# The gated rows of the one-hot matrices: one VectorE compare-and-multiply per token instead of a compare and a ScalarE scaling

## The chip, the cores and the metric

The program runs on one core of a Trainium2 chip. A core has TensorE (PE: matrix products, with a weight load PEld ahead of each), VectorE (DVE), ScalarE (ACT), GpSimd (POOL) and SyncE (SP, which here only issues transfers); 16 DMA engines move data between HBM and the on-chip memory SBUF. TensorE writes its results to PSUM. The metric is the device time of one execution in microseconds, lower is better.

## The reference, cut to what matters

Two transformer blocks run over 512 tokens of width 1024 (retention, sliding-window attention, then latent and differential attention). The change concerns the last part, a mixture of 16384 one-neuron experts (`peer_ffn`). For every token and each of 8 heads it picks 16 experts; an expert number is made of two halves below 128, and each pick has a gate `g`.

```
cand = sv[:, :, 0, :, None] + sv[:, :, 1, None, :]
fv, fpos = lax.top_k(cand, PEER_TOPK)
eidx = jnp.take_along_axis(cidx, fpos, axis=-1)      # first half * 128 + second half
g = jax.nn.softmax(fv, axis=-1)
a = jax.nn.gelu(jnp.einsum('ted,td->te', u_tab[eidx], hb))
return jnp.einsum('te,ted->td', g * a, v_tab[eidx])
```

## The kernel before, in words

The first 1050 us are the attention layers, the next 180 the router's scores and the first picks. What matters here is the stretch from about 1230 to 1770 us of the profile, called the gate stage below, and the 560 us behind it, the V stage.

Tokens come in four tiles of 128. Tile 0's experts are gathered row by row: `gather` (L1239, an indirect DMA issued by POOL) fetches one row per token, and `weigh` (L1248, VectorE) multiplies it with the token. For the other three tiles (384 tokens, 96 groups of four) TensorE works out the activations of all experts, 128 at a time, and a dense matrix of gates, which the V stage multiplies together before the sum over experts.

In the gate stage one loop runs over `n`, the 96 groups of four tokens. For each n it records, in this order: `one_hots(n + 4)`, some pieces of `finalize` (top-16 picks, gates and numbers of the next tile, L1139 to L1207), about 1.03 steps of `u_mm` and `u_prep`, 1.33 gathers and weighings, and `dense_gates(n)`.

- `u_prep` prepares the table rows of 128 experts: a load on SP's queue (L1044, two experts' blocks, 1 MB), a rounded copy `hi` on ScalarE (L1052), and the rest `lo` = raw - hi (L1056), in turn on VectorE (one step) and on POOL (two halves). `u_mm` is 24 products `pa` on TensorE (L94), then a gelu on ScalarE (L1071, `gsp`) which also frees the PSUM buffer (there are two), and a store `Ad` on SP's queue.
- `one_hots` builds, for four tokens, two matrices with a row per pick: entry (row, i) is one where i equals the half of the pick's number, and in the second matrix it is the gate instead of one. VectorE compares the row of numbers 0 to 127 (`io`) with both halves of all four tokens in one step of 128x1024 (L1213, `junk`), then ScalarE multiplies the second matrix of each token by its gates (L1216, four steps of 128x128).
- `dense_gates` multiplies the two matrices of each token on TensorE (`att`, four products) and copies the result on ScalarE (L1230) into staging buffers, written to HBM (`Gd`, L1232) every eighth n. The staging buffers and the loads of `u_prep` share four buffers, `raw`.

The order on PE and on DVE is the order of the loop (`manual_schedule`); the orders on ACT, POOL and SP come from the framework's scheduler, which may place them anew when instructions go. There are four `junk` buffers, so one_hots(n + 4) waits for the products of dense_gates(n). The loop is

```
lr[n + AQ] = one_hots(n + AQ)
...
    u_mm()
    u_prep(nc.vector if nl % 2 else nc.gpsimd)
gathers(NG1 * (n + 1) / NQ)
...
dense_gates(n, lr.pop(n))
```

Of the kernel before, what the change touches and what calls it, by code (L numbers as in the profile page):

```python
# [31 lines left out]
def consts():  # L32
    """Tables that depend on the shapes alone."""
    f = np.float32
    out = {}
    ang = (1.0 / (f(10000.0) ** np.linspace(0.0, 1.0, 128, dtype=f))).astype(f)
    pos = np.arange(S, dtype=f)
    a = (pos[None, :] * ang[:, None]).astype(f).astype(np.float64)
    out["xcos"] = np.cos(a).astype(f)
    out["xsin"] = np.sin(a).astype(f)  # L40
    gam = 1.0 - 2.0 ** (-5.0 - np.arange(4, dtype=np.float64))
    diff = np.arange(S)[None, :] - np.arange(P)[:, None]
    dec = np.where(diff[:, None, :] >= 0, gam[None, :, None] ** np.maximum(diff, 0)[:, None, :], 0.0) / 16.0
    out["dec"] = dec.astype(f)
    half = 32
    inv = (1.0 / (f(10000.0) ** (np.arange(half, dtype=f) / f(half)))).astype(f)
    a = (np.arange(S, dtype=f)[:, None] * inv[None, :]).astype(f).astype(np.float64)
    out["rcos"] = np.cos(a).astype(f)
    out["rsin"] = np.sin(a).astype(f)
    d = np.arange(384) - 127  # L50
    dd = np.maximum(d, 0)
    big = 16 + (np.log(np.maximum(dd, 1).astype(f) / f(16)) / f(math.log(128 / 16)) * f(16)).astype(np.int32)
    bucket = np.where(dd < 16, dd, np.minimum(big, 31))
    oh = np.zeros((64, 384), f)
    ok = (d >= 0) & (d < 128)
    for u in range(384):
        if ok[u]:
            oh[bucket[u], u] = 1.0
        else:
            oh[32, u] = NEG  # L60
    out["oneh"] = oh
    out["cmask"] = np.where(np.arange(P)[None, :] <= np.arange(P)[:, None], 0.0, NEG).astype(f)
    out["iota"] = np.broadcast_to(np.arange(P, dtype=f), (P, P)).copy()
    starts = np.cumsum([0] + [16 // (a + 1) for a in range(15)])
    out["iota16"] = np.broadcast_to(np.stack([np.arange(16), starts]).astype(f), (P, 2, 16)).copy()
    return out
# [3 lines left out]
def tile_kernel(ctx: ExitStack, tc: tile.TileContext, I: dict, out: bass.AP):  # L70
# [41 lines left out]
    def rstd(ss, n, inv, eps=EPS, tag="rs"):  # L112
        """(ss * inv + eps) ** -0.5 for [P, n]."""
        m = sm.tile([P, 8], F32, tag="ms", name=nm("ms"))
        r = sm.tile([P, 8], F32, tag=tag, name=nm("rs"))
        nc.gpsimd.tensor_scalar(m[:, :n], ss, inv, eps, op0=OP.mult, op1=OP.add)
        last_rstd[0] = nc.gpsimd.tensor_tensor(r[:, :n], m[:, :n], mhalf[:, :n], op=OP.pow).ins
        return r
# [44 lines left out]
    def wchunk(*a, **kw):  # L163
        """Weights [nk k-tiles, n columns] as exact high and low float32r parts, a list of
        (hi, lo) by k-tile. parts: list of (dram AP [nk*128, c], column offset)."""
        for ks in wload(*a, **kw):
            pass
        return ks

    def gemm_tok(xh, xl, ks, n, t):  # L170
        """psum [128 tokens of tile t, n] = x^T . W"""
        ps = pmm.tile([P, 512], F32, tag="mm", name=nm("mm"))
        nk = len(ks)
        for k, (h, l) in enumerate(ks):
            xs = slice(t * P, (t + 1) * P)
            mm(ps[:, :n], xl[:, k, xs], h[:, :n], k == 0, False)
            mm(ps[:, :n], xh[:, k, xs], l[:, :n], False, False)
            mm(ps[:, :n], xh[:, k, xs], h[:, :n], False, k == nk - 1)
        return ps

    def gemm_T(xh, xl, ks, c0):
        """psum [128 columns of W from c0, all tokens]"""
        ps = pmm.tile([P, 512], F32, tag="mm", name=nm("mm"))
        nk = len(ks)
        cs = slice(c0, c0 + P)
        for k, (h, l) in enumerate(ks):
            mm(ps, l[:, cs], xh[:, k, :], k == 0, False)
            mm(ps, h[:, cs], xl[:, k, :], False, False)
            mm(ps, h[:, cs], xh[:, k, :], False, k == nk - 1)
        return ps  # L190

    def gemm_half(ps, xh, xl, ks, c0, t2):
        """As gemm_T, for two of the tiles of tokens."""
        xs = slice(t2 * 256, t2 * 256 + 256)
        cs = slice(c0, c0 + P)
        nk = len(ks)
        for k, (h, l) in enumerate(ks):
            mm(ps[:, xs], l[:, cs], xh[:, k, xs], k == 0, False)
            mm(ps[:, xs], h[:, cs], xl[:, k, xs], False, False)
            mm(ps[:, xs], h[:, cs], xh[:, k, xs], False, k == nk - 1)  # L200
# [7 lines left out]
    def to_T(src, n, th, tl, t, k0=0):  # L208
        """Transposes src [128 tokens, n*128] into th/tl[:, k0.., tile t]."""
# [24 lines left out]
    def col_vec(ap, n, name):  # L234
        """A vector of n*128 as [128, n], element k*128+p at (p, k)."""
        tl = cst.tile([P, n], F32, name=name)
        nc.gpsimd.dma_start(tl, ap.rearrange("(k p) -> p k", p=P))
        return tl

# [32 lines left out]
    def mod_gain(g_ap, sh_row, sc_row, raw=None):  # L272
        """Row 0: gain * (1 + scale), row 1: shift."""
# [18 lines left out]
    with ExitStack() as sa:  # L292
# [32 lines left out]
        # small vectors and tables of the later stages, loaded when the norms are done  # L325
# [43 lines left out]
        def small():  # L369
            # attention bias by distance, to be read back one row per query  # L370
# [10 lines left out]
            # -lambda on every partition  # L381
# [12 lines left out]
        def a_qk(h):  # L394
            # q, k with the pairs of a rotation in two blocks
# [34 lines left out]
        def a_scores(h, qT, kT):  # L430
            # decayed scores, keys on the partitions
# [71 lines left out]
    with ExitStack() as sb:  # L503
# [53 lines left out]
        def b_scores(g, t, hf, bt, qT, rq):  # L557
            """Softmax of 4 heads, not yet divided by its sum."""
# [99 lines left out]
    with ExitStack() as sc_:  # L658
# [19 lines left out]
        # rope tables with the gains in them: [P, tile, 64] for cos and for sin with its sign  # L678
        tabs = {}

        def rope(dst, src, name, t, n):
            """dst, src [P, n, 64] (normalised, gain not yet applied)."""
# [41 lines left out]
        # rotary key and differential v  # L724
# [15 lines left out]
        def latent(name, c0, nb, lh, ll):  # L740
            """Latents, transposed, and the reciprocal rms of each token."""
# [13 lines left out]
        # latent queries, keys and values  # L755
# [98 lines left out]
        def c_scores(i, h):  # L854
            """Weights of the keys for heads 0..3 (latent, to be divided by the sum) and 4..7."""
# [35 lines left out]
        def c_end(i, h, po, rl4):  # L891
# [4 lines left out]
            else:  # L896
                # rms over a head, where a sum of squares beyond float32's range gives zero
# [14 lines left out]
        # short rows of scores next to long ones  # L912
# [58 lines left out]
        def r_scores(hp, qT, sk, s):  # L971
            """Scores of a half of a head's keys, and the 16 largest."""
# [9 lines left out]
        for c in range(2):  # L982
            cs = slice(c * 512, (c + 1) * 512)
            ks = wchunk([(I["w_out_2"][0][:, cs], 0)], KT, 512, [None] * 4 + [gsub[:, 0:1]] * 4)
            if c == 1:
                gsh = mod_gain(I["norm2_g_2"][0], 3, 4, pc.tile([P, 2 * D], F32, tag="qnT", name="gsh2"))
                # the router's first head fills the wait for the last norm
# [24 lines left out]
    # Tile 0's experts are gathered row by row; for the other tiles all experts' activations  # L1012
    # are worked out on the tensor engine, and weighted by a dense matrix of gates.
# [3 lines left out]
    # activations kept on chip, and rows under way  # L1017
    LA = 14
    NGR = 4
    # the other activations are kept in DRAM  # L1020
# [13 lines left out]
    # activations of all experts, 128 of them (one first half) at a time  # L1034
# [95 lines left out]
    # pairs (a, b) of the two sorted halves that can be among the 16 largest sums  # L1130
    PAIRS = [(0, 1, 16), (1, 2, 8), (2, 3, 5), (3, 4, 4), (4, 5, 3), (5, 8, 2), (8, 16, 1)]

    def finalize(t):
        """Gates and the two halves of the expert numbers, [tokens, slots]; in pieces."""
# [29 lines left out]
        # steps from one a to the next, of its number and of 128 times its first position  # L1164
# [44 lines left out]
    def one_hots(n):  # L1209
        """Both halves of 4 tokens' numbers as rows of ones and zeros, the first times the gates."""  # L1210
        src, tk = iT[n * 4 // P], n * 4 % P
        LR = junk().rearrange("p (e t n) -> p e t n", e=2, t=4)
        nc.vector.tensor_tensor(LR, io.unsqueeze(1).unsqueeze(1).to_broadcast([P, 2, 4, P]),  # L1213
                                src[:, 0:2, tk:tk + 4].unsqueeze(3).to_broadcast([P, 2, 4, P]), op=OP.is_equal)
        for i in range(4):
            nc.scalar.activation(LR[:, 1, i], LR[:, 1, i], AF.Copy, scale=src[:, 2, tk + i:tk + i + 1])  # L1216
# [4 lines left out]
    def dense_gates(n, LR):  # L1221
        """For 4 tokens, [second half of the number, first half]; written by 32."""
# [35 lines left out]
    # shared out over the steps  # L1258
# [3 lines left out]
    def gathers(n, pool_ins=None, dve_ins=None):  # L1262
        """Gathers rows until n of them are under way, and weighs those of the last call."""
# [125 lines left out]
    def step(j):  # L1389
        """Ahead: the loads of a later j; then the sums over this j's experts."""  # L1390
# [17 lines left out]
    with tc.manual_schedule(engines={mybir.EngineType.PE}):  # L1408
# [15 lines left out]
        # the last sums by tile, so that only the last tile's end is left  # L1424
# [12 lines left out]
def layouts(inputs):  # L1437
    """Inputs once more, in another order of their elements."""
# [24 lines left out]
```

## Time and profile before

| what | value |
|---|---|
| median of 3 runs | 2336.23 us (2334.72 to 2336.91) |
| span of the profiled execution, first to last instruction | 2333.6 us |
| busy in the span | PE 2230.1 us (96%), DVE 1587.2 (68%), ACT 984.4 (42%), POOL 767.1 (33%) |
| mean granted TensorE clock | 0.984 of full speed |

Of the profiled execution the span alone is given; the runs of the table are timed without a profile, and their median lies 2.6 us above it. Busy times are averages over stages; which engine a stage waits for is read from that stage. "Start to start" below is the distance between the starts of two neighbouring instructions of one engine: on VectorE the next one's start is shown some 0.08 us before the end of the one ahead of it, so this distance, not the duration, is what an instruction costs in a full queue.

### The profile page before, as it was taken

The page shows a single profiled execution, that of the slowest core. Times are in us where ns is not written, and L with a number is a line of the kernel's source. Part 1 is how long each engine was busy: PE and PEld are TensorE (multiplying, and loading weights), DVE is VectorE, ACT ScalarE, POOL GpSimd, SP SyncE. Part 2 cuts the span into 40 slices and gives each one's busy share as a digit, 9 for nine tenths or more (in the row PEclk, how much of TensorE's full clock was granted, in tenths as well). Part 3 has the DMA queues.
Part 4 walks back from the last instruction along what each step waited for, and adds up shares of the span by engine and source line. Part 5 has one row for each costly group of instructions (what it writes and reads, how often), then busy time and mean ns, then how long its engine had stood idle before and what let it go on. Part 6 is the DMA issues. An engine that isn't in the chain of part 4 may idle for free.

```text
span 2333.6 us, 31094 instructions
## 1 busy us (share of the span) xinstructions
PE 2230.1 (96%) x11343; PEld 1913.5 (82%) x11343; DVE 1587.2 (68%) x2929; ACT 984.4 (42%) x1972; POOL 767.1 (33%) x683
## 2 busy tenths in 40 slices
PE   7999999998989999989999989989999999999999
PEld 6777777787878775678989989989998888888887
DVE  5664545346366665559788797787775888787778
ACT  4213132245353545433436656566653333333332
POOL 4211111111101340000584675585563333222222
PEclk9999999999999999899999999999999999999999
DMA  7754544321212221123346889879999999999995
GB/s 222 188 169 103 155 114 126 90 91 55 72 45 72 91 69 40 43 77 118 118 149 234 325 281 337 294 280 331 333 338 320 354 347 344 343 336 333 337 312 179
DMA packets 226600, 476.33 MB, mean 204 GB/s; under 512 B 15504, under 2 KB 118352, under 8 KB 223376
## 3 DMA queue, kind: packets, MB, share of 16 engines
q1 hardware_dynamic: 121904, 291.79, 37.0%
q0 software_dynamic: 38160, 134.90, 16.7%
q10 hardware_dynamic: 66384, 47.67, 6.7%
q8 instruction: 89, 1.46, 0.2%
q14 instruction: 63, 0.52, 0.1%
HBM read 424.58 MB, written 49.73 MB: 203 GB/s over the span
## 4 chain that ended last, share of the span: by engine, by line
PE 78%; DVE 9%; DMA 6%; ACT 2%; POOL 2%; issue 2%; SPq 0%; POOLq 0%; DVEq 0%; ACTq 0%
PE mm L94 27%; PE acc L94 23%; PE pa L94 16%; PE att L94 9%; DMA ada<-in_ada_w_dram 3%; PE tp L97 2%; DMA raw<-in_peer_u_T_dram 2%; DVE junk L264 1%; DVE junk L1213 1%; DMA Gd<-raw 1%; DVE gr L1248 1%; DVE wlo L125 1%; POOL lo L1056 1%; PE po L94 1%; DVE lo L1056 1%
## 5 line engine op out<-in xcount | busy, mean ns | idle before, releaser
L94 PE MATMUL pa<-xTh,lo 128*128 128x384 f32 x1024 | 357.6, 349 | 25.8 <-POOL lo L1056 11.7
L94 PE MATMUL pa<-xTh,hi 128*128 128x384 f32 x1024 | 348.6, 340 | 0.0
L94 PE MATMUL pa<-xTl,hi 128*128 128x384 f32 x1024 | 348.3, 340 | 0.0
L94 PE MATMUL acc<-hi,cl 128*128 128x512 f32 x768 | 303.8, 396 | 0.5 <-DVE cl L125 0.5
L94 PE MATMUL acc<-lo,ch 128*128 128x512 f32 x768 | 303.7, 396 | 0.0
L94 PE MATMUL acc<-hi,ch 128*128 128x512 f32 x768 | 303.7, 396 | 0.0
L1056 POOL TENSOR_TENSOR lo<-raw,hi 128x512 fp32r<-128x512 f32 x158 | 230.8, 1485 | 200.3 <-ACT hi L1052 198.1
L1239 POOL DMA_INDIRECT gr<-in_peer_v_dram,ei x128 | 158.6, 1239 | 375.2 <-DVE y L1256 361.6
L94 PEld LDWEIGHTS pa<-xTh,lo 128*128 128x128 f32 x1024 | 194.8, 190 | 29.7 <-issue 15.3
L94 PE MATMUL mm<-whi,xTl 128*128 128x512 f32 (+2 forms) x544 | 210.0, 386 | 7.5 <-DVE junk L721 2.6
L124 ACT CAST ch<-ga 128x384 fp32r<-128x384 f32 x128 | 65.6, 513 | 344.0 <-PE acc L94 335.3
L94 PE MATMUL mm<-wlo,xTh 128*128 128x512 f32 (+2 forms) x544 | 206.6, 380 | 0.5 <-DVE wlo L125 0.5
L94 PE MATMUL mm<-whi,xTh 128*128 128x512 f32 (+2 forms) x544 | 206.9, 381 | 0.0
L1239 POOL DMA_INDIRECT gr<-in_peer_u_dram,ei x128 | 162.3, 1268 | 123.1 <-DVE gr L1248 105.6
L1213 DVE TENSOR_TENSOR junk<-io,iTa 128x1024 f32<-128x1024 f32 x96 | 147.4, 1539 | 73.2 <-PE att L94 64.5
L94 PEld LDWEIGHTS pa<-xTl,hi 128*128 128x128 f32 x1024 | 194.9, 190 | 0.0
L94 PEld LDWEIGHTS pa<-xTh,hi 128*128 128x128 f32 x1024 | 194.1, 190 | 0.0
L125 DVE TENSOR_TENSOR wlo<-wraw,whi 128x1024 fp32r<-128x1024 f32 (+3 forms) x99 | 120.7, 1232 | 79.4 <-ACT whi L124 79.2
L94 PEld LDWEIGHTS acc<-hi,cl 128*128 128x128 f32 x768 | 144.3, 188 | 35.8 <-DVE cl L125 0.9
L94 PEld LDWEIGHTS acc<-lo,ch 128*128 128x128 f32 x768 | 144.3, 188 | 34.9
L94 PEld LDWEIGHTS acc<-hi,ch 128*128 128x128 f32 x768 | 144.3, 188 | 34.8
L1299 DVE TENSOR_TENSOR lo<-raw,hi 128x1024 fp32r<-128x1024 f32 x128 | 156.5, 1222 | 23.8 <-ACT hi L1298 22.9
(384 smaller groups left out, 4664.1 us busy)
## 6 DMA issues: line engine op xcount, KB each, us to landing
raw<-in_peer_u_T_dram SPq DMA_DIRECT2D x64, 1024.0 KB
raw<-in_peer_v_dram SPq DMA_DIRECT2D x64, 1024.0 KB
ada<-in_ada_w_dram SPq DMA_DIRECT2D x48, 512.0 KB
Gd<-raw SPq DMA_DIRECT2D x24, 1024.0 KB
G<-Gd ACTq DMA_DIRECT2D x31, 768.0 KB
Ad<-gsp SPq DMA_DIRECT2D x114, 192.0 KB
ga<-Ad ACTq DMA_DIRECT2D x114, 192.0 KB
wraw<-in_a_w_in_dram SPq DMA_DIRECT2D x16, 1024.0 KB
```

The source lines that it names most:

```text
L94: return nc.tensor.matmul(o, l, r, start=a, stop=b).ins
L97: nc.tensor.transpose(o, s, ident)
L124: nc.scalar.copy(hi, src)
L125: return nc.vector.tensor_tensor(lo, src, hi.bitcast(F32), op=OP.subtract).ins
L264: nc.vector.scalar_tensor_tensor(acc, raw[:, k, :], s, acc, op0=OP.mult, op1=OP.add)
L1056: ins = eng.tensor_tensor(ul[:, es], raw[:, es], uh[:, es].bitcast(F32), op=OP.subtract).ins
L1213: nc.vector.tensor_tensor(LR, io.unsqueeze(1).unsqueeze(1).to_broadcast([P, 2, 4, P]), src[:, 0:2, tk:tk + 4].unsqueeze(3).to_broadcast([P ...
L1239: nc.gpsimd.indirect_dma_start(out=r, out_offset=None, in_=I["peer_u_2" if which == 0 else "peer_v_2"][0], in_offset=bass.IndirectOffsetOn ...
L1248: nc.vector.scalar_tensor_tensor(r, r, 1.0, hy, op0=OP.mult, op1=OP.mult, accum_out=acoef[:, j:j + 1])
L1299: ins = nc.vector.tensor_tensor(vl, raw, vh.bitcast(F32), op=OP.subtract)
```

## The change

The step on both halves becomes a step on the first half alone, and the second half is made by four VectorE steps, one for each token, each a compare with the number (a value per partition) and a multiplication with the gate (a second value per partition). ScalarE's four steps go. The rest of the diff removes comments, and all lines behind L1213 move down by one.

```
     LR = junk().rearrange("p (e t n) -> p e t n", e=2, t=4)
-    nc.vector.tensor_tensor(LR, io.unsqueeze(1).unsqueeze(1).to_broadcast([P, 2, 4, P]),
-                            src[:, 0:2, tk:tk + 4].unsqueeze(3).to_broadcast([P, 2, 4, P]), op=OP.is_equal)
+    nc.vector.tensor_tensor(LR[:, 0], io.unsqueeze(1).to_broadcast([P, 4, P]),
+                            src[:, 0, tk:tk + 4].unsqueeze(2).to_broadcast([P, 4, P]), op=OP.is_equal)
     for i in range(4):
-        nc.scalar.activation(LR[:, 1, i], LR[:, 1, i], AF.Copy, scale=src[:, 2, tk + i:tk + i + 1])
+        nc.vector.tensor_scalar(LR[:, 1, i], io, src[:, 1, tk + i:tk + i + 1], src[:, 2, tk + i:tk + i + 1],
+                                op0=OP.is_equal, op1=OP.mult)
     return LR
```

VectorE's queue in the middle of tile 2's `finalize` (`lk`, `i`, `fp` and `pos` are its tables, `gr` a gathered row, `lo` a rest for TensorE), before:

```order
L1179 TENSOR_TENSOR lk_11457<-pos_11241,io_7835 128x1024
L1248 SCALAR_TENSOR_TENSOR gr_11438,acoef<-gr_11438,hy 128x1024
L1248 SCALAR_TENSOR_TENSOR gr_11440,acoef<-gr_11440,hy 128x1024
L1213 TENSOR_TENSOR junk_11506<-io,iTa 128x1024
L1185 TENSOR_REDUCE i_2206_11351<-lk_11457 128x64
L1190 CAST fp_10419<-i_2206_11351 128x128
L1191 TENSOR_SCALAR fp_10419<-fp_10419 128x128
L1194 CAST i_2233_11515<-fp_10419 128x128
L1195 SCALAR_TENSOR_TENSOR i_2206_11351<-i_2233_11515,i_2206_11351 128x128
L1196 TENSOR_TENSOR pos_11241<-pos_11241,i_2233_11515 128x128
L1179 TENSOR_TENSOR lk_11519<-pos_11241,io_7835 128x1024
L1056 TENSOR_TENSOR lo_11551<-raw_11488,hi_11550 128x1024
```

The same place after the change:

```order
L1179 TENSOR_TENSOR lk_11457<-pos_11241,io_7835 128x1024
L1249 SCALAR_TENSOR_TENSOR gr_11438,acoef<-gr_11438,hy 128x1024
L1249 SCALAR_TENSOR_TENSOR gr_11440,acoef<-gr_11440,hy 128x1024
L1213 TENSOR_TENSOR junk_11506<-io,iTa 128x512
L1216 TENSOR_SCALAR junk_11506<-io,iTa 128x128 x4
L1185 TENSOR_REDUCE i_2206_11351<-lk_11457 128x64
L1190 CAST fp_10419<-i_2206_11351 128x128
L1191 TENSOR_SCALAR fp_10419<-fp_10419 128x128
L1194 CAST i_2233_11515<-fp_10419 128x128
L1195 SCALAR_TENSOR_TENSOR i_2206_11351<-i_2233_11515,i_2206_11351 128x128
L1196 TENSOR_TENSOR pos_11241<-pos_11241,i_2233_11515 128x128
L1179 TENSOR_TENSOR lk_11519<-pos_11241,io_7835 128x1024
```

One instruction of twice the width became five; the instructions around it stand in the same order, and so they do on the whole queue. PE's order is the same throughout.

ScalarE's queue later in the gate stage (`hi` is a rounded copy of a loaded `raw`, `gsp` a gelu that frees the PSUM buffer `pa`, the copies to `raw` are those of `dense_gates`), before:

```order
L1071 ACTIVATE gsp_13049<-pa_13024 128x384
L1230 COPY raw_13005<-att_13059 128x64x4
L1230 COPY raw_13006<-att_13059 128x64x4
L1216 ACTIVATE junk_13014<-junk_13014,iTa 128x128 x4
L1071 ACTIVATE gsp_13097<-pa_13072 128x384
L1230 COPY raw_13005<-att_13112 128x64x4
L1230 COPY raw_13006<-att_13112 128x64x4
L1052 CAST hi_13102<-raw_13100 128x1024
L1052 CAST hi_13157<-raw_13100 128x1024
L1216 ACTIVATE junk_13066<-junk_13066,iTa 128x128 x4
L1071 ACTIVATE gsp_13154<-pa_13129 128x384
```

The same place after the change:

```order
L1071 ACTIVATE gsp_13049<-pa_13024 128x384
L1231 COPY raw_13005<-att_13059 128x64x4
L1231 COPY raw_13006<-att_13059 128x64x4
L1052 CAST hi_13102<-raw_13100 128x1024
L1071 ACTIVATE gsp_13097<-pa_13072 128x384
L1052 CAST hi_13157<-raw_13100 128x1024
L1231 COPY raw_13005<-att_13112 128x64x4
L1231 COPY raw_13006<-att_13112 128x64x4
L1071 ACTIVATE gsp_13154<-pa_13129 128x384
```

The scalings are gone, and the first copy of raw_13100 now stands ahead of the gelu gsp_13097 instead of behind it.

## Rows read from the trace of the kernel before

**Rows 1.** Busy us by stretch (--windows): stretch, length, engines (instructions), granted clock, DMA.

```profile
1331.00:1382.00 51.00, 44.55 (x271) 44.15 (x270) 50.61 (x51) 28.49 (x72) 41.40 (x25) 0.97 0.77 277
1382.00:1517.00 135.00, 132.67 (x824) 131.94 (x823) 103.87 (x187) 79.79 (x193) 82.38 (x59) 1.00 0.87 312
1517.00:1548.00 31.00, 27.93 (x163) 27.80 (x164) 30.35 (x29) 19.09 (x48) 28.22 (x16) 0.94 0.68 231
1548.00:1770.00 222.00, 218.22 (x1343) 217.72 (x1343) 149.68 (x170) 130.89 (x313) 130.35 (x101) 0.99 0.92 335
1770.00:2300.00 530.00, 526.18 (x2277) 426.19 (x2276) 420.92 (x496) 184.71 (x253) 159.88 (x130) 1.00 0.96 331
```

**Rows 2.** Waits of PE, 1225 to 1770 us: total us, times, longest.

```profile
PE pa L94 <- POOL lo L1056: 7.1, 5, 3.2
PE pa L94 <- DVE lo L1056: 5.9, 3, 4.8
PE pa L94 <- ACT gsp L1071: 3.6, 1, 3.6
```

**Rows 3.** Groups by line, 1225 to 1760 us: busy us, mean ns | idle before, releasers.

```profile
L1213 DVE TENSOR_TENSOR junk<-io,iTa 128x1024 f32<-128x1024 f32 x96 | 147.4, 1539 | 73.2 <-PE att L94 64.5 <-ACT iTa L1207 4.6 <-PE pa L94 3.2
...
L1216 ACT ACTIVATE junk<-junk,iTa 128x128 f32<-128x128 f32 x384 | 122.9, 394 | 59.7 <-DVE junk L1213 58.7 <-issue 0.6
```

**Rows 4.** Line L1213: duration ns min/median/max, first and last start us.

```profile
L1213 DVE TENSOR_TENSOR junk<-io,iTa x96: 1212/1226/6030, 1230.2 to 1726.8; 128x1024 f32<-128x1024 f32 x96
```

**Rows 5.** VectorE's timeline early on: start us, us, line, operation.

```profile
52.89 0.47 DVE L262 TENSOR_SCALAR junk<-ada,sc_sb 128x512 f32<-128x512 f32 x1
53.29 0.21 DVE L361 CAST cmb<-cmf 128x128 bf16<-128x128 f32 x1
...
480.74 0.68 DVE L125 TENSOR_TENSOR xTl<-tp,xTh 128x512 fp32r<-128x512 f32 x1
481.33 0.22 DVE L693 TENSOR_SCALAR sg_kpe<-sg_kpe 128x128 f32<-128x128 f32 x1
481.47 0.22 DVE L693 TENSOR_SCALAR sg_qpe<-sg_qpe 128x128 f32<-128x128 f32 x1
481.60 0.75 DVE L454 TENSOR_SCALAR junk<-x_sb,rs 128x1024 f32<-128x1024 f32 x1
482.27 0.60 DVE L522 TENSOR_SCALAR junk<-mm,rs 128x128 f32<-128x128 f32 x2
```

**Rows 6.** VectorE's timeline, 1345 to 1377 us.

```profile
1345.59 1.21 DVE L1213 TENSOR_TENSOR junk<-io,iTa 128x1024 f32<-128x1024 f32 x1
1346.73 1.21 DVE L1185 TENSOR_REDUCE i<-lk 128x64 f32<-128x1024 f32 x1
...
1353.47 1.42 DVE L1213 TENSOR_TENSOR junk<-io,iTa 128x1024 f32<-128x1024 f32 x1
...
1356.05 0.26 DVE L1190 CAST fp<-i 128x128 int32<-128x128 f32 x1
...
1356.61 2.99 DVE L1194 CAST i<-fp 128x128 f32<-128x128 int32 x1
...
1361.30 1.22 DVE L1056 TENSOR_TENSOR lo<-raw,hi 128x1024 fp32r<-128x1024 f32 x1
...
1376.11 1.22 DVE L1213 TENSOR_TENSOR junk<-io,iTa 128x1024 f32<-128x1024 f32 x1
```

**Rows 7.** POOL's timeline beside Rows 6.

```profile
1357.00 2.50 POOL L1056 TENSOR_TENSOR lo<-raw,hi 128x512 fp32r<-128x512 f32 x2
```

**Rows 8.** The chain that ended last, in order of time: start us, us, what.

```profile
1380.42 1.28 POOL lo L1056
...
1521.23 5.95 DVE junk L1213
```

**Rows 9.** ScalarE's timeline at the longest wait for a load.

```profile
1505.09 0.49 ACT L1071 ACTIVATE gsp<-pa 128x384 f32<-128x384 f32 x1
...
1515.42 1.99 ACT L1052 CAST hi<-raw 128x1024 fp32r<-128x1024 f32 x2 [9.31 <-DMA raw<-in_peer_u_T_dram]
```

## The prediction

> **What bounds the kernel now.** I read the stretches first, then TensorE's waits, then the instructions inside the two stretches where TensorE waits. By stretch, TensorE is busy 218 of 222 us and 526 of 530 us late in the gate stage and in the V stage, so nothing that only relieves another engine can be seen there. It falls short in two places, 1331 to 1382 us (44.6 of 51) and 1517 to 1548 us (27.9 of 31), and exactly there VectorE is full: 50.6 of 51 and 30.4 of 31 [rows 1]. In both, tile 2 or tile 3 is at the look-up part of `finalize`, on top of the steady work. TensorE's waits in the whole gate stage come to 7.1 + 5.9 + 3.6 = 16.6 us, for `lo` from POOL, `lo` from VectorE, and a late gelu [rows 2]. That is all that a faster side could return, apart from the low clock behind a long wait: the granted clock is 0.97 over the 51 us and 0.94 over the 31 us [rows 1], 0.03 x 51 = 1.5 us and 0.06 x 31 = 1.9 us of lost speed.
>
> ScalarE spends 122.9 us on the 384 scalings and sits 58.7 us idle ahead of them until VectorE's compare is done [rows 3], but it is busy only 28.5 of 51 and 19.1 of 31 us in the two short stretches [rows 1]. The engine that the change relieves is not the one that these stretches wait for; the one that it loads is.
>
> **The change part by part.**
>
> *Price of one group of four tokens on VectorE.* Now: one step, from 1345.59 to the next start at 1346.73, 1.14 us [rows 6]. Then: one step of 512 and four of 128. A two-input step of 512 takes 0.59 us start to start (480.74 to 481.33) [rows 5]; I take 0.60. For a compare and multiplication by two values per partition there is no row. With no such value, 128 elements take 0.13 to 0.14 us (481.33, 481.47, 481.60) [rows 5]. With one, 512 take 0.40 (52.89 to 53.29) and 1024 take 0.67 (481.60 to 482.27) [rows 5], so 0.27 for 512 elements, 0.07 for 128, and 0.13 fixed: 0.20. Without a value per partition the fixed part is 0.135 - 0.07 = 0.065, so one value costs about 0.065. Two of them: 0.26, which is my value; it is also what the nearest row with 128 elements and one value has (two in 0.60 us, the last one's end shown some 0.08 late) [rows 5]. [...] The sum is 0.60 + 4 x 0.26 = 1.64, so +0.50 us a group; the ends are 0 and +0.78.
>
> *Waits for POOL.* The compare lasts 1.226 us at its median and 6.03 at most; its mean of 1.539 means that it loses 0.31 us each time on average [rows 3, 4], and in the trace these losses fall where POOL has a `lo` or `lk` step. Five instructions have five starts at which POOL can be ahead. The nearest row is a single-input cast of 128: 0.26 us at 1356.05, and 2.99 us for the next such cast at 1356.61, behind POOL's two halves of 2.50 us from 1357.00 [rows 6, 7]. So a group may lose 2.7 us more (one pair of halves inside each), or 0.3 us less (its wait goes, as the long hold is split). I take +0.5: nearer to the mean loss that this same step has, 0.31, than to the pair, because one pair of halves can hold back several of the five starts at once.
>
> [...]
>
> *What lies on the path.* Groups inside the two full stretches delay TensorE one for one, since VectorE has no gap there. Up to the `lo` of 1361.30, for which TensorE waited 4.8 us [rows 2, 6], there are four groups after the stretch's start at 1331 (the last at 1353.47); up to POOL's `lo` of 1380.42, which stands behind gathers that need VectorE's weighings, four more (the last at 1376.11) [rows 6, 8]; in the second stretch four, the first at 1521.23 [rows 8]. Twelve groups x (0.50 + 0.50) = +12.0 us.
>
> The other 84 groups are hidden: VectorE is busy 103.9 of 135 us between the two stretches and 149.7 of 222 us after them [rows 1]. For the 25 groups in the 135 us, 25 us more meet 31 us of idle; tight, and gone if the price is higher. The V stage has none of these steps.
>
> *ScalarE's side.* A group's four scalings take 122.9 / 96 = 1.3 us of its queue [rows 3]. Ahead of the second stretch that lets the gates' store and the load behind it start 1.3 us earlier: -1.3 us. Against it stands the move in ScalarE's queue that the order shows. The copy of the next load now stands ahead of a gelu that ran at 1505.09, and the load came at 1515.42 after 9.31 us of waiting [rows 9]. One copy (half of 1.99 us) and the gelu (0.49) later it is about 1517, and TensorE, which needs that gelu's PSUM buffer, has stopped earlier than before and has work left over from then. VectorE's full stretch begins with the second copy's `lo`, one gelu (0.5 us) later, and TensorE waits for VectorE at its end anyway, so of this I count only the gelu's +0.5 us. Together -0.8. No other ScalarE wait is on the path: the remaining waits of its copies are for loads, which scalings don't delay.
>
> *Clock.* The second wait of the first stretch, one of the five for POOL's `lo`, grows by its four groups, 4 us, to the size of the longest waits of today, 4.8 and 3.6 us [rows 2]. The two stretches that hold these are the ones with the low granted clock [rows 1], so I add what the first stretch loses by it now: +1.5 us.
>
> *Sum.* 12.0 - 0.8 + 1.5 = +12.7 us on a span of 2333.6, with 2.6 us around it: 2349 us, 12.7 above the median of the runs, 2336.2.
>
> **The rivals.**
>
> *No difference: the short steps are cheap.* If two values per partition cost nothing (0.135 us a step) and no wait is added, a group costs 0.60 + 0.54 = 1.14 us, what it costs now. VectorE's stretches stay as they are, and -0.8 is left: 2335.4 us. For it: the rows of 0.13 us [rows 5]. Against it: each row with a value per partition has a larger fixed part. [...]
>
> *Faster: ScalarE was the hidden link.* VectorE's compare, late behind POOL, holds ScalarE's queue for 58.7 us in all [rows 3], and behind it stand the copies `hi`, the gelus and the copies whose stores must land before loads can start. If loads and copies come that much earlier, the wait of 3.6 us for a gelu closes, and of the 7.1 us for POOL I count half, since part of them lies behind VectorE [rows 2]; with the first goes the clock's 1.9 us [rows 1]: 3.6 + 3.6 + 1.9 = 9 us, 2327. It decides where VectorE's addition stays under 0.3 us a group. Against it: in the two full stretches ScalarE waits for VectorE, not VectorE for it, and where loads are late ScalarE is already waiting for them [rows 9].
>
> *Much slower: POOL gets in between.* If every second group loses a pair of halves, 1.35 instead of 0.5 us, twelve groups cost 12 x 1.85 = 22 us, and the 25 groups of the stretch between need 46 us where 31 are idle, of which I count half of the 15 us over: 2336.2 + 22 + 7.5 - 0.8 + 1.5 = 2366. For it: POOL is busy 41.4 of 51 and 28.2 of 31 us in the full stretches [rows 1]. Against it: the wide compare has the same POOL beside it and loses 0.31 us.
>
> **How the numbers follow.** Chances: the forecast 0.42, no difference 0.20, faster 0.21, much slower 0.17. A change of less than 0.2% (4.7 us) can't be told from none here, which makes 2331.6 to 2340.9 the middle. Slower takes the forecast but for 0.02, and the third rival: 0.57. Same takes 0.18 of the second case and 0.02 of the forecast: 0.20. Faster takes 0.21 and the other 0.02: 0.23. The range goes from just above the faster case to just above the much slower one, 2329 to 2367; the forecast's own range is 2342 to 2356.
>
> **What would show it.** Right: the compare of 512 at about 0.68 us, the four steps at 0.26 us start to start where POOL is quiet and one in several at over 1 us where it is not; VectorE's total up by about 50 us plus waits; TensorE's waits for `lo` up from 7.1 + 5.9 = 13 us to some 25, and the end of the gate stage near 1783 us. Wrong: the two stretches no longer than before, or TensorE's 16.6 us of waits going down. If the steps take under 0.15 us, the price was wrong; if they take 0.26 and TensorE's waits still fall, the path was.

## The result and the profile after

The changed kernel is slower: 2359.6 us in the median of its first four runs (2350.9 to 2364.0) against 2336.6 us, a ratio of 1.0092 with a 95% interval of 1.0067 to 1.0116, or +21.5 us (15.7 to 27.1). Two more sets of it, 1.0083 (1.0055 to 1.0111) and 1.0078 (1.0057 to 1.0100), give +19.4 and +18.2 us. The forecast was slower by 12.7 us, at 2349 us in 2329 to 2367. The first median also lies above the forecast's own range (2342 to 2356), inside the whole one. Single runs of either kernel spread over 9 to 25 us in a set, so below every difference comes from the ratio of a set's runs to those of before in the same set, with its interval, and a trace shows how the time of one run is made up.

The trace of after has a span of 2349.1 us, 15.5 more than before; its run (2350.9 us) is the shortest of the four. By stretch (columns as in [rows 1]):

```profile
1331.00:1382.00 51.00, 43.41 (x256) 42.71 (x256) 48.86 (x69) 18.29 (x34) 35.37 (x23) 0.93 0.75 261
1382.00:1517.00 135.00, 127.06 (x781) 126.36 (x780) 124.18 (x288) 51.62 (x98) 72.55 (x58) 0.97 0.82 290
1517.00:1548.00 31.00, 25.89 (x149) 25.70 (x148) 26.24 (x37) 10.82 (x21) 20.92 (x14) 0.89 0.67 240
1548.00:1770.00 222.00, 217.70 (x1350) 217.38 (x1349) 177.67 (x332) 84.55 (x165) 122.47 (x99) 0.99 0.91 328
```

VectorE's work went up from 103.9 to 124.2 us in the 135 us between the two full stretches, and from 149.7 to 177.7 behind them [rows 1], ScalarE's down by a third. TensorE lost 1 to 6 us in the first three stretches, and the granted clock is lower in each of them. (The windows stand at the same times in both traces, while the work in them comes up to 11 us later after the change.) Its waits, 1225 to 1785 us, against [rows 2]:

```profile
PE pa L94 <- DVE lo L1056: 11.5, 4, 5.9
PE att L97 <- DVE i L1185: 6.4, 1, 6.4
PE pa L94 <- ACT gsp L1071: 5.1, 1, 5.1
PE pa L94 <- POOL lo L1056: 2.9, 3, 1.4
PE pa L94 <- ACT raw L1231: 0.5, 1, 0.5
```

VectorE's share rose from 5.9 to 17.9 us, and a wait is new: TensorE's transposition of `i`, which `finalize` makes at the end of the look-up. The two lines that answer to [rows 4]:

```profile
L1213 DVE TENSOR_TENSOR junk<-io,iTa x96: 678/691/3875, 1231.5 to 1740.0; 128x512 f32<-128x512 f32 x96
...
L1216 DVE TENSOR_SCALAR junk<-io,iTa x384: 327/340/3341, 1232.2 to 1741.4; 128x128 f32<-128x128 f32 x192
```

A gated step takes 0.34 us at its median and 3.34 at most. What that is in a full queue is seen on VectorE's timeline, answering to [rows 6]:

```profile
1350.89 0.68 DVE L1213 TENSOR_TENSOR junk<-io,iTa 128x512 f32<-128x512 f32 x1
1351.49 1.10 DVE L1216 TENSOR_SCALAR junk<-io,iTa 128x128 f32<-128x128 f32 x4
1352.52 1.21 DVE L1185 TENSOR_REDUCE i<-lk 128x64 f32<-128x1024 f32 x1
...
1378.53 0.69 DVE L1213 TENSOR_TENSOR junk<-io,iTa 128x512 f32<-128x512 f32 x1
1379.14 4.11 DVE L1216 TENSOR_SCALAR junk<-io,iTa 128x128 f32<-128x128 f32 x4
...
1384.31 0.68 DVE L1213 TENSOR_TENSOR junk<-io,iTa 128x512 f32<-128x512 f32 x1
1384.91 4.00 DVE L1216 TENSOR_SCALAR junk<-io,iTa 128x128 f32<-128x128 f32 x4
1388.83 1.21 DVE L1185 TENSOR_REDUCE i<-lk 128x64 f32<-128x1024 f32 x1
```

And POOL beside it:

```profile
1380.09 2.55 POOL L1056 TENSOR_TENSOR lo<-raw,hi 128x512 fp32r<-128x512 f32 x2
...
1385.81 2.49 POOL L1056 TENSOR_TENSOR lo<-raw,hi 128x512 fp32r<-128x512 f32 x2
```

The group of 1350.89 is the undisturbed one: 0.60 + 1.03 = 1.63 us until the next instruction starts, 0.257 us a step. In the groups of 1378.53 and 1384.31 one of the four steps lasts from before POOL's pair of halves starts (a gather runs on POOL until then) to its end, 3.34 and 3.23 us, and a group takes 4.6 and 4.5 us. The instruction behind the second, the last reduction of the look-up, starts at 1388.83; before it was 1377.25:

```profile
1377.25 1.21 DVE L1185 TENSOR_REDUCE i<-lk 128x64 f32<-128x1024 f32 x1
```

This is what the transposition waits for. The shift between the two traces, read from the gelus and products of each table step, is +0.2 us at 1306 us of before, +10.6 at 1407, still +10.6 at 1480, +13.3 from 1583 to 1750, and +16.3 at 1777.

### The profile page after: what moved, and what is told of

Same layout as the page of the kernel before. It is cut to its first block, busy times and chain, and to the rows that moved or that the text cites. A ratio compares the mean times of both kernels' runs of the same rounds, so it can differ in the third digit from the quotient of the medians.

```text
span 2349.1 us, 31096 instructions
## 1 busy us (share of the span) xinstructions
PE 2232.8 (95%) x11343; PEld 1916.9 (82%) x11343; DVE 1642.8 (70%) x3313; ACT 870.7 (37%) x1588; POOL 733.2 (31%) x683
## 4 chain that ended last, share of the span: by engine, by line
PE 75%; DVE 11%; DMA 7%; ACT 2%; issue 2%; POOL 2%; SPq 0%; DVEq 0%; POOLq 0%; ACTq 0%
PE mm L94 26%; PE acc L94 22%; PE pa L94 16%; PE att L94 9%; DMA ada<-in_ada_w_dram 4%; PE tp L97 2%; DVE junk L1216 1%; DVE junk L264 1%; DVE gr L1249 1%; DMA raw<-in_peer_u_T_dram 1%; DMA Gd<-raw 1%; DVE wlo L125 1%; DVE junk L1213 1%; PE po L94 1%; POOL lo L1056 1%
## 5 line engine op out<-in xcount | busy, mean ns | idle before, releaser
L1240 POOL DMA_INDIRECT gr<-in_peer_u_dram,ei x128 | 137.0, 1070 | 152.1 <-DVE gr L1249 135.5
L1052 ACT CAST hi<-raw 128x1024 fp32r<-128x1024 f32 x128 | 132.3, 1048 | 93.9 <-DMA raw<-in_peer_u_T_dram 89.4
```

The costliest lines, as they stand in the source:

```text
L1052: nc.scalar.copy(uh, raw)
L1240: nc.gpsimd.indirect_dma_start(out=r, out_offset=None, in_=I["peer_u_2" if which == 0 else "peer_v_2"][0], in_offset=bass.IndirectOffsetOn ...
```

## The experiments

In the table the twelve groups are n = 23 to 30 and 56 to 59, those in VectorE's full stretches; their VectorE time is taken start to start from each trace, idle time left out. TensorE's waits and the time that it lost at half speed (granted clock 0.50, as from 1391 to 1394 us behind the 6.4 us wait of the first trace: products 0.30 to 0.34 us apart instead of 0.16 to 0.18, 0.16 us each) are those of the gate stage of the same trace, from the 534th to the 3024th of the 3072 products `pa`. The length of this stretch without the two is 525 to 528 us in all of them (532 with the steps doubled), so the two terms hold nearly all of its differences. A microsecond figure of the third column is the ratio's distance from 1 times the median of before of that set. Of the kernel before there is one trace, from the first set, whose median of before (2336.6) is 3.7 to 6.2 us above those of the later sets; 24.9 us is that one trace's draw, and the two runs that keep the old compare in the twelve groups (no scaling, new form in the other 84) have 17.9 and 22.3.

| kernel | ratio (95%) | us against before | twelve groups, us | waits + half speed, us |
|---|---|---|---|---|
| before | | | 24.9 | 16.6 + 4.6 |
| changed, first trace | 1.0092 (1.0067 to 1.0116) | +21.5 | 43.6 | 28.3 + 6.7 |
| changed, second | 1.0083 (1.0055 to 1.0111) | +19.4 | 31.8 | 14.5 + 4.2 |
| changed, third | 1.0078 (1.0057 to 1.0100) | +18.2 | 39.3 | 26.1 + 10.2 |
| no scaling | 0.9985 (0.9969 to 1.0001) | -3.5 | 17.9 | 11.1 + 3.4 |
| new form in the other 84 | 1.0013 (0.9994 to 1.0032) | +3.0 | 22.3 | 17.6 + 5.4 |
| new form in the twelve | 1.0063 (1.0042 to 1.0085) | +14.7 | 38.8 | 25.8 + 4.8 |
| gated steps doubled | 1.0434 (1.0410 to 1.0458) | +101 | 53.6 | 88.9 + 33.6 |
| gated steps read PSUM | 1.0016 (1.0002 to 1.0030) | +3.7 | 30.0 | 15.4 + 5.8 |
| gated half on ScalarE, twelve | 0.9995 (0.9981 to 1.0010) | -1.2 | 20.7 | 10.6 + 1.4 |
| two wide steps | 1.0089 (1.0060 to 1.0118) | +20.7 | 32.0 | 24.7 + 9.4 |
| before, compare reads PSUM | 0.9942 (0.9924 to 0.9960) | -13.5 | 13.8 | 4.4 + 2.7 |
| the same and the look-ups | 0.9931 (0.9911 to 0.9951) | -16.1 | 13.8 | 1.3 + 0.0 |
| changed, all steps read PSUM | 0.9963 (0.9948 to 0.9979) | -8.6 | 22.6 | 9.0 + 1.4 |

**The changed kernel again, twice.** No edit.

> The changed kernel once more, for its spread: its four runs lie between 2350.9 and 2364.0 us, those of before between 2334.7 and 2343.4, and the trace is of the shortest, 2350.9 (span 2349.1, +15.5). Whatever the cause, the median should come to 2351 to 2364 us. If the trace taken here is of a longer run, the stretch that the surplus lies in should be one of the two in which VectorE is full (tile 2's or tile 3's finalize) by the theory that VectorE's waits for POOL vary from run to run; by the rival that transfers vary, it lies in the V stage or at a wait for a load.

> The changed kernel a third time, for another trace: its two traces so far are of its shortest runs, with 43.6 and 31.8 us for VectorE's twelve groups (24.9 before) and +15.5 and -1.0 us of span. Expected from theory A1: again 0.26 us a step where POOL is quiet, some 25 of 384 steps late by over 0.25 us, at other groups than before; the span follows the waits in the twelve groups. The median +16 to +22 against before.

Medians 2349.9 (2334.4 to 2359.0) and 2349.4 us (2338.4 to 2352.6). The first lies below the expected 2351 to 2364, with a median of before that is lower too (2332.9); the ratio agrees. Late steps (over 0.25 us above the median) are 25, 25 and 31 of 384 in the three traces, with 38, 37 and 55 us above the median in all, and every one of them overlaps a `lo` or `lk` step of POOL. Of the steps that start while POOL runs one of these (16, 20 and 18) none is on time. The late steps fall in part at the same places: of the 18 groups with a late step in the first trace 9 have one in the second too and 14 in the third, for which other groups were expected. The gate stage (the stretch of the table) lasts 562.9, 544.9 and 564.1 us, so it holds nearly all of the differences of the three spans, 2349.1, 2332.6 and 2348.1 us. The second trace, of the shortest run of all, waits only 0.8 us where the others wait 6.4 and 5.2 (TensorE's waits of the second, then of the third):

```profile
PE pa L94 <- DVE lo L1056: 8.6, 2, 5.9
PE pa L94 <- POOL lo L1056: 4.6, 4, 2.2
PE pa L94 <- ACT gsp L1071: 1.4, 1, 1.4
...
PE att L97 <- DVE i L1185: 0.8, 1, 0.8
```

```profile
PE pa L94 <- POOL lo L1056: 8.5, 5, 4.3
PE pa L94 <- DVE lo L1056: 7.1, 3, 6.0
PE pa L94 <- ACT gsp L1071: 5.5, 2, 5.0
PE att L97 <- DVE i L1185: 5.2, 1, 5.2
```

So the price of 0.26 us is the same in all three, and the waits change from run to run: (twelve groups - 24.9) / 12 - 0.49 gives 1.07, 0.08 and 0.71 us a group.

**ScalarE's side alone.**

```
-        for i in range(4):
-            nc.scalar.activation(LR[:, 1, i], LR[:, 1, i], AF.Copy, scale=src[:, 2, tk + i:tk + i + 1])
```

> The kernel before with ScalarE's four scalings left out (the gates are then not in the second matrix) and VectorE's wide compare as it was: ScalarE's side of the change alone, with the order that ScalarE then gets. Theory A (VectorE's twelve groups in its two full stretches set the time): the time of before within 4 us, about -1. Theory C (the new order on ScalarE, whose gelu wait went from 3.6 to 5.1 us, makes a good part of the loss): +5 us or more. If ScalarE's scalings were the hidden link: -9.

-3.5 us (-7.2 to +0.2), not told apart from nothing. ScalarE's relief doesn't make the loss, and at its best returns a few microseconds. But ScalarE's order isn't that of the changed kernel here: at the late load, whose copy the change puts ahead of a gelu, the gelu stays ahead, and TensorE waits 0.2 us for gelus in all. So this run doesn't test the new order (theory C); the next one does. In its trace VectorE's twelve groups lose less to waits, 17.9 us instead of 24.9; whether that is the relief or the draw of one run, it doesn't say.

**Which groups count.** Two counterparts. The edit is that of the first, with the old form in the twelve; the second has the two branches exchanged.

```
+    PATH = (*range(23, 31), *range(56, 60))
...
+        if n in PATH:
+            nc.vector.tensor_tensor(LR, io.unsqueeze(1).unsqueeze(1).to_broadcast([P, 2, 4, P]),
...
+                nc.scalar.activation(LR[:, 1, i], LR[:, 1, i], AF.Copy, scale=src[:, 2, tk + i:tk + i + 1])
+        else:
+            nc.vector.tensor_tensor(LR[:, 0], io.unsqueeze(1).to_broadcast([P, 4, P]),
...
+                nc.vector.tensor_scalar(LR[:, 1, i], io, src[:, 1, tk + i:tk + i + 1], src[:, 2, tk + i:tk + i + 1],
```

> The new form in 84 of the 96 groups, the old one (one compare, four ScalarE scalings) in the twelve that lie in VectorE's full stretches: n = 23 to 30 and 56 to 59. Theory A: the time of before within 4 us. Theory B (VectorE's added work counts wherever it stands, in proportion): 84/96 of the loss, +14 to +20 us. Theory C: the loss or most of it, since ScalarE is relieved and reordered nearly everywhere.

> The counterpart: the new form in the twelve groups n = 23 to 30 and 56 to 59 alone, the old form in the other 84. Theory A: nearly the whole loss, +12 to +20 us (twelve groups of +0.49 us price and +0.5 to +1.1 us of waits for POOL). Theory B: 12/96 of the loss, +2 to +3 us. Theory C: under +4 us.

84 new groups cost +3.0 us (-1.4 to +7.5), twelve new groups +14.7 (9.8 to 19.8). In proportion to their number it would have been 17 and 2. Both come out as theory A says. TensorE's waits with the twelve:

```profile
PE pa L94 <- DVE lo L1056: 10.7, 3, 6.0
PE pa L94 <- POOL lo L1056: 7.9, 3, 6.0
PE att L97 <- DVE i L1185: 6.4, 1, 6.4
```

and with the 84:

```profile
PE pa L94 <- POOL lo L1056: 6.9, 6, 2.2
PE pa L94 <- ACT gsp L1071: 6.0, 2, 5.5
PE pa L94 <- DVE lo L1056: 4.6, 3, 3.6
```

The transposition's wait is there with the twelve and gone with the 84, which keep VectorE's waits at 4.6 us (5.9 before). The 84 also have ScalarE's new order at the late gelu, and its 5.5 us: what that order costs, ScalarE's relief counted against it, is within their +3.0 (at most 7.5). The twelve keep the order of before there, wait 0.8 us for gelus, and still lose 14.7 us.

**The gated steps doubled.**

```
-        for i in range(4):
+        for i in (0, 1, 2, 3) * 2:
```

> The changed kernel with its four gated steps made twice over (the same values written again). They cost 0.257 us each from start to start in the trace, so a group costs 1.03 us more. Theory A (VectorE's twelve groups in its full stretches set the time): 12 x (1.03 + 0 to 0.6 of further waits) = +12 to +20 us above the changed kernel, and the 25 groups between the two stretches no longer fit either: VectorE has 135 - 124 = 11 us idle there and would need 26 to 33, +15 to +22. Together +27 to +42 above the changed kernel, +45 to +60 above the kernel before. If VectorE does not set the time: less than +10 above the changed kernel.

+101 us against before, or some 80 to 83 above the changed kernel, about twice what was expected. By stretch (columns as in [rows 1]):

```profile
1331.00:1385.00 54.00, 38.37 (x216) 37.72 (x215) 47.33 (x112) 16.49 (x30) 20.80 (x17) 0.91 0.64 223
1385.00:1520.00 135.00, 113.18 (x638) 112.15 (x638) 134.25 (x301) 39.94 (x79) 59.94 (x47) 0.88 0.73 253
1520.00:1550.00 30.00, 25.71 (x143) 25.39 (x142) 29.69 (x76) 9.79 (x20) 14.16 (x12) 0.89 0.66 209
1550.00:1775.00 225.00, 201.28 (x1178) 199.83 (x1177) 223.59 (x466) 77.61 (x149) 114.34 (x88) 0.94 0.78 275
```

VectorE is now full in the last 225 us too. The expectation had counted the groups between the stretches but not the 36 behind them, where after had 222 - 177.7 = 44 us of idle and up to 36 x (1.03 + 0.6) = 59 were added. The steps added are 96 x 1.03 = 99 us. From the first group to the last VectorE's idle time falls from 54 to 9 us, so 45 us of them fill gaps; against that the late steps went from 25 to 54 (of 768), and their excess from 38 to 100 us. With VectorE full nearly everywhere the added work counts in groups that were hidden before, and the waits grow with it.

**The same steps with an input in PSUM.** The copy is made once.

```
+    iop = piop.tile([P, P], F32, name="iop")
+    nc.scalar.copy(iop, io)
...
-            nc.vector.tensor_scalar(LR[:, 1, i], io, src[:, 1, tk + i:tk + i + 1], src[:, 2, tk + i:tk + i + 1],
+            nc.vector.tensor_scalar(LR[:, 1, i], iop, src[:, 1, tk + i:tk + i + 1], src[:, 2, tk + i:tk + i + 1],
```

> The changed kernel with the row of numbers (io) that the four gated steps read copied to PSUM once; the compare of 512 still reads SBUF. [...] They cost 0.30 us instead of 0.26 (the nearest row with a PSUM input), a group 0.60 + 1.20 - 1.14 = +0.66 us, twelve of them +8, less 2 us of waits that the shorter compare saves: +3 to +10 us above before. Theory A2 (the price alone, the waits only change places): no gain from it, a little dearer than the changed kernel: +17 to +24 above before.

+3.7 us (0.5 to 7.0) where the changed kernel has +18 to +21. The line of the gated steps:

```profile
L1219 DVE TENSOR_SCALAR junk<-iop,iTa x384: 392/402/414, 1230.8 to 1728.1; 128x128 f32<-128x128 f32 x192
```

A step is dearer, 0.32 us start to start, and none of 384 is late: 0.41 us at most. More VectorE work per group (1.88 against 1.63 us) and a shorter kernel: it comes out as theory A1 says, by which a good part of the loss is gated steps that wait while POOL runs (the +3 to +10 us is its range), and not as A2 does, and the waits were the larger part. One thing is not held fixed: with the added copy ScalarE's queue keeps the order of before at the late gelu, whose wait (5.1, 1.4 and 5.0 us in the changed kernel) is absent here. Some of the gain may be that, up to what the 84 groups cost; the kernel before with its compare in PSUM, below, leaves no such doubt.

**The opposite of the change in the twelve groups.**

```
+            nc.vector.tensor_tensor(LR[:, 0], io.unsqueeze(1).to_broadcast([P, 4, P]),
+                                    src[:, 0, tk:tk + 4].unsqueeze(2).to_broadcast([P, 4, P]), op=OP.is_equal)
+            for i in range(4):
+                nc.scalar.activation(LR[:, 1, i], io, AF.Abs, bias=src[:, 1, tk + i:tk + i + 1], scale=-1.0)
+                nc.scalar.activation(LR[:, 1, i], LR[:, 1, i], AF.Relu, bias=src[:, 2, tk + i:tk + i + 1],
...
```

The scale of the second step, left out of the lines above, is the negative gate from a table of 48 columns.

> The opposite of the change, in the twelve groups n = 23 to 30 and 56 to 59 only: VectorE makes just the compare of 512, and ScalarE makes the gated half by itself, in two steps a token: the distance |io - number|, then relu(gate - gate x distance). The other 84 groups are those of before. Theory A: VectorE saves 1.14 - 0.60 = 0.54 us a group, 6.5 us in all, and some of its waits for POOL, against four more ScalarE steps (1.2 us) a group on an engine that is busy 28 of 51 and 19 of 31 us there: -3 to -9 us against before. Theory C (ScalarE's queue decides, gelus come later): 0 to +5.

-1.2 us (-4.4 to +2.3): less than theory A's -3 to -9, though the interval reaches into it, and into theory C's 0 to +5; this run decides nothing between them. VectorE did save 4.2 us in the twelve groups, and TensorE still waits:

```profile
PE pa L94 <- DVE lo L1057: 6.7, 3, 3.0
PE pa L94 <- POOL lo L1057: 5.2, 5, 1.7
PE pa L94 <- ACT gsp L1072: 1.5, 2, 1.2
```

Taking 0.54 us off a group doesn't take the waits for POOL away: three of the twelve groups still lose 2.4 us or more. Where the rest of the saving went is open.

**Two wide steps instead of five.** The wide compare is that of before.

```
+        nc.vector.tensor_tensor(LR[:, 1], LR[:, 1], src[:, 2, tk:tk + 4].unsqueeze(2).to_broadcast([P, 4, P]), op=OP.mult)
```

> The whole gated half on VectorE in two steps instead of five: the wide compare of before (1.14 us), then one two-input multiplication of 512 by the gates (0.60). No ScalarE scaling. The price is 1.74 us a group, 0.11 above the changed kernel, but there are two starts at which POOL can be ahead instead of five. Theory A1 (the number of starts makes the waits): +0.60 x 12 = 7 us and 0 to 0.3 us of waits a group: +7 to +11 us above before, below the changed kernel's +17 to +21. Theory A2 (the price alone, or work of this length meets POOL as often in two pieces as in five): as the changed kernel or 1 us more, +17 to +23.

+20.7 us (14.0 to 27.5), as the changed kernel, where A1 had +7 to +11. Fewer and longer steps are no better. Yet VectorE's twelve groups did what the form of A1 that counts starts says of them: 32.0 us, +7.1, which is the price alone. So, by the one trace of before, two thirds of the loss lie outside them, and how they arise is not shown. Two things differ in the trace. VectorE's idle time ahead of the twelve groups (n below 23) is 3.9 us, 10.1 in the changed kernel and 18.9 before, so its full stretch begins earlier. And POOL is slower at the gathers (the second number between the bars is the mean in ns), here and then in before:

```profile
L1238 POOL DMA_INDIRECT gr<-in_peer_u_dram,ei x124 | 173.1, 1396 | 117.7 <-DVE gr L1247 100.5 <-issue 13.2 <-PE pa L94 0.6
```

```profile
L1239 POOL DMA_INDIRECT gr<-in_peer_u_dram,ei x124 | 158.3, 1276 | 121.5 <-DVE gr L1248 105.6 <-issue 6.8 <-PE att L94 3.4
```

A gather takes 1.40 us beside these steps, 1.28 before and 1.07 in the changed kernel. That this wide compare, with both inputs in SBUF, holds POOL's gathers up, the next run shows: with one input in PSUM they take 0.99 us instead of the 1.28 of before.

**The kernel before, its compare reading PSUM.**

```
-        nc.vector.tensor_tensor(LR, io.unsqueeze(1).unsqueeze(1).to_broadcast([P, 2, 4, P]),
+        nc.vector.tensor_tensor(LR, iop.unsqueeze(1).unsqueeze(1).to_broadcast([P, 2, 4, P]),
```

> The kernel before (wide compare, ScalarE scalings) with the row of numbers that the wide compare reads copied to PSUM once. In the kernel before that compare loses 30.3 us to waits in 96 groups, 24.9 - 12 x 1.14 = 11.2 us of it in the twelve groups of the full stretches. Theory A1 (a step with an input in PSUM doesn't wait while POOL runs, and the waits in the twelve groups are time on the path): no compare over 1.4 us, and -5 to -11 us against before. Theory A2 (the waits only change places, the next SBUF step waits instead): within 3 us of before.

> The last kernel, and the small tables that finalize's look-up compares (lk, 1.14 us, 3.3 us where it waits) read are in PSUM too. Theory A1: a further 0 to 3 us below the last kernel, as one lk step in each full stretch waits 2 us today. Theory A2: as the last kernel.

-13.5 us (-17.7 to -9.3) and, with the look-up's tables in PSUM as well, -16.1 (-20.7 to -11.4); the two aren't told apart by time. The first is more than A1's -5 to -11 in its middle. ScalarE's order around the late gelu is that of before in both, and still the 3.6 us for it are gone. The compare's line in the first of them against [rows 4], where the longest lasted 6.03 us, TensorE's waits against [rows 2], and the gathers:

```profile
L1216 DVE TENSOR_TENSOR junk<-iop,iTa x96: 1210/1223/1226, 1228.7 to 1710.5; 128x1024 f32<-128x1024 f32 x96
```

```profile
PE pa L94 <- DVE lo L1056: 3.1, 1, 3.1
PE pa L94 <- POOL lo L1056: 1.2, 2, 0.9
```

```profile
L1242 POOL DMA_INDIRECT gr<-in_peer_u_dram,ei x124 | 123.1, 992 | 134.8 <-DVE gr L1251 121.7 <-issue 6.0 <-PE pa L94 1.2
```

The same step at the same 1.22 us, none late, and a gather back at 0.99 us. Of TensorE's 16.6 us of waits 4.3 are listed here; with the look-ups in PSUM too it is 1.2:

```profile
PE pa L94 <- POOL lo L1056: 1.2, 2, 0.9
```

Both engines wait less, and these runs don't part the two. Theory A2, that the waits only change places, falls. Of the look-up compares in the full stretches of before one was late, 3.30 us at 1347.97; the two in the second stretch took 1.23 and 1.25 us.

**The change without its waits.** Both edits on the changed kernel: the compare of 512 and the gated steps read `iop`.

> The changed kernel with both kinds of its steps, the compare of 512 and the four gated ones, reading the row of numbers from PSUM: the change at its bare price. A group is 0.60 + 4 x 0.32 = 1.88 us, +0.75 against before, twelve of them +9 us, less the 11.2 us of waits that before has in them. Theory A1: -2, that is -5 to +3 us against before. Theory A2: as the changed kernel with the gated steps alone in PSUM, +1 to +7.

-8.6 us (-12.1 to -4.9), below A1's range of -5 to +3 by its middle, and clear of A2's +1 to +7; no step is late:

```profile
L1216 DVE TENSOR_TENSOR junk<-iop,iTa x96: 677/685/693, 1226.6 to 1712.5; 128x512 f32<-128x512 f32 x96
...
L1219 DVE TENSOR_SCALAR junk<-iop,iTa x384: 393/401/409, 1227.2 to 1714.1; 128x128 f32<-128x128 f32 x192
```

As in the run with the gated steps alone in PSUM, ScalarE's order at the late gelu is not that of the changed kernel, and there is no wait for it. Against the kernel before with its compare in PSUM the kernel is 13.5 - 8.6 = 4.9 us slower, for 22.6 - 13.8 = 8.8 us more in the twelve groups (the two intervals overlap, so the 4.9 is a rough size). So the change, with the waits out of it, costs some 5 us, ScalarE's 123 us of relief included; made as it was, it costs 18 to 21.

## Why the prediction was right, and where it was too small

*What bounds.* Right. The twelve groups carry +14.7 of +18 to +21 us, the other 84 +3.0 (7.5 at most). The 25 groups between the stretches were hidden, as forecast: the shift stays at +10.6 us there.

*Price.* Right to the hundredth: 0.257 us a step against 0.26, a group +0.49 against +0.50. That each value costs 0.065 us, from which 0.26 was worked out, no run tests. The upper end of +0.78 us a group had 0.33 us a step, for which no row or run shows the source; a step with the input in PSUM takes 0.32 us, which makes a group +0.74. The lower end and the rival of no difference needed 0.135 us.

*Waits for POOL.* The term of 0.5 us a group came out at 1.07, 0.08 and 0.71 in three traces, 0.62 in the mean, inside its ends of -0.3 and 2.7; against the one trace of before, whose own twelve groups wait 11.2 us. A value so spread was hit in the middle by luck. In the first trace a group thus costs 1.56 us, between the forecast's 1.0 and the 1.85 of the much slower rival; that rival's mechanism is there, a pair of halves inside a group: 6, 1 and 5 of the twelve groups take over 4 us in the three traces, 1 before. So its every second group is right in two traces, and only the waits that before already had keep the sum below it. That short steps are held up as well is shown by the late ones, of 3.3 us at most where the median is 0.34, and by their absence once the row of numbers is in PSUM: 0 of 384 gated steps, and 0 of 96 wide compares in the kernel before, are late.

*Path.* Right in place, and partly wrong in the name. By the end of the first stretch the shift was +10.6 us (forecast 8 x 1.0 and 1.5 for the clock), by the second a further 2.7 (forecast 4.0 - 0.8). That this is so close is luck: in the second trace the shift grew by 2.2 us over the first stretch and fell by 3.9 up to the end of the second, in the third it grew by 12.5 and 5.3. Of the 2.7 us in the first trace 1.9 came up at the late gelu and 0.1 over the second stretch itself, so what its four groups did alone is not shown. And TensorE's second wait in the first stretch was not for POOL's `lo`: it was the transposition behind VectorE's last reduction, 6.4 us. So its waits for `lo` came to 14.4 us in the view above, hardly more than the 13 of before, where the prediction had some 25 as a sign of being right. In the second trace its waits are even below those of before (14.5 against 16.6 us), a sign of being wrong by the prediction's own words; by the medians the kernel is slower all the same. The end of the stage was near 1786 us (forecast 1783); 3 us of that came up behind 1750, where I had nothing, in the first trace alone.

*ScalarE's side.* Forecast -0.8. The relief without the new order measures -3.5 with an interval that holds 0; the wait for the late gelu, where the order is new, went from 3.6 to 5.1, 1.4 and 5.0 us; for that order the prediction had +0.5. The faster rival's 9 us are excluded.

*Clock.* Forecast +1.5 us. Half-speed time went from 4.6 to 6.7, 4.2 and 10.2 us. In the first trace the granted clock fell in the stretch between, too (0.97 after 1.00), behind the 6.4 us wait at its start.

*The size.* The effect is 18 to 21 us and I forecast 12.7, below the interval's lower end in all three sets, if barely in two. The terms that were too small in two of the three traces are the waits for POOL and the low clock behind long waits; the gelu's wait may be a third. In the third trace, whose run is at the median of its set, the twelve groups are 14.4 us longer (forecast 12.0) and the half-speed time 5.6 (1.5). How much each adds to the median can't be read from three traces of runs that differ by 15 us.

## What to carry to other kernels

Price a step that moves to VectorE twice: by its start-to-start time, and by what it does in the stretches where VectorE is full and GpSimd works beside it; here the second was the larger in two of three traces, and it varied from run to run. When steps with two SBUF inputs, or small ones, are found several times longer than their median beside GpSimd work (here the wide compare 6.03 us against 1.23, a gated step 3.34 against 0.34), look first for a small input that can live in PSUM: a row of 128 numbers there took 13.5 us off the kernel before and turned the change from +18 to +21 into -8.6, in part perhaps through ScalarE's order. Work added to an engine counted where that engine was full (+14.7 us from the twelve groups there, +3.0 from the other 84); enough of it filled the gaps elsewhere, and then it counted there too (99 us of added steps cost 80 to 83).

## What was not expected of the hardware

A gated step takes 0.257 us with its input in SBUF and 0.32 us from PSUM, but the wide compare takes 1.22 us from either, so the move to PSUM is free for the one and not for the other. The disturbance goes both ways: the gathers on GpSimd, which these VectorE steps share no data with, took 1.28 us beside the wide SBUF compare, 1.07 beside the compare of 512 and four short steps, 1.40 beside the wide compare and a multiplication of 512, and 0.99 with the row in PSUM. And the same program ran from 2334 to 2359 us in one set, and waited 6.4, 0.8 and 5.2 us at the same transposition in its three traces.
